# The second MLP's u turned by transposing DMAs, as two planes of 16-bit halves, in a two-layer decoder trunk on one Trainium2 core

## The chip, the core and the metric

The kernel runs on one core of one Trainium2 chip. The core has five engines that work at the same time, each through its own list of instructions in order: TensorE (PE, matrix products; its weight loads are listed apart as PEld), VectorE (DVE), ScalarE (ACT), GpSimd (POOL) and SyncE (SP), which here issues the DMAs. An instruction that needs another engine's result waits for a semaphore, and everything behind it on its engine waits too. Data lies in SBUF (128 partitions); TensorE writes its sums to PSUM, which ScalarE and VectorE can read and a DMA cannot.

The metric is the time of one execution on the device in microseconds (us); lower is better. A profiled execution is one execution with its trace: when each instruction ran, and what it waited for.

## The reference

Two layers work on x (256 tokens x 2048 features, float32). Layer 0 mixes tokens with a convolution module, layer 1 with differential attention; each is followed by the same kind of MLP with hidden width 8192. The change touches the MLP of layer 1 alone:

```python
def squared_relu_mlp(h, w1, b1, w2, b2):
    u = jnp.square(jax.nn.relu(h @ w1 + b1))
    return u @ w2 + b2
...
    for i in range(DEPTH):
        ...
        x = layer_norm(DEEPNORM_ALPHA * x + g_m * y, ln_mix_g[i], ln_mix_b[i])
        h = x * (1.0 + sc_f) + sh_f
        y = squared_relu_mlp(h, mlp_w1[i], mlp_b1[i], mlp_w2[i], mlp_b2[i])
        x = layer_norm(DEEPNORM_ALPHA * x + g_f * y, ln_ffn_g[i], ln_ffn_b[i])
```

The scales, shifts and gates (sc, sh, g) come from an adaptive layer norm: products of a condition vector with the rows of a large matrix (`ada_w`), which the kernel computes in between, on VectorE.

## The kernel before

**Products.** Each large product is made of three: both factors are split into a high part that TensorE multiplies at full speed (type fp32r) and a low part, the rest. high x high, high x low and low x high are summed in PSUM (lines 700, 702 and 703). The weights come from HBM in tiles of 1 MB (2048 numbers on each of the 128 partitions, line 636). A tile is worked on in two halves of 1024: ScalarE casts a half to its high part `wh` (line 655), VectorE subtracts to get the low part `wl` (line 657), and TensorE does 12 matmuls with it (2 blocks of 128 rows, 2 blocks of 128 tokens, 3 products). There are four buffers for raw tiles (`N_RAW`), shared with the rows of the adaLN matrix, and four pairs of buffers for split halves (`N_SP`).

**The MLP** (`mlp`, called with i = 1 for the second). The hidden width is worked on in four quarters q. A quarter has four groups g of w1 (512 hidden columns each, 4 tiles, 8 halves), which fill u for this quarter, and then four groups n of w2, each over the quarter's 2048 rows (again 4 tiles, 8 halves). A group's sum lies in two PSUM banks, one for each block of 128 tokens, t = 0 and 1.

**Turning u.** A w1 group leaves u with tokens on the partitions; w2 needs it with hidden features there. When a bank of a w1 group is done, `on_t1` runs: ScalarE copies it to SBUF (`us`, line 1452), and `rest` is put off by `U_WAIT` = 2 ticks. Then TensorE makes four 128x128 transposes into a PSUM bank (`ut`, line 1458). In the second MLP VectorE adds the bias b1 (line 1471) and makes the square of the positive part (line 1474), both to `r`; ScalarE casts `r` to u's high part (`u_hi`, line 513) and VectorE subtracts for the low part (`u_lo`, line 516), in `put_split`. Both u buffers hold a whole quarter.

**What sets the order.** `run_jobs` writes the program half by half. Before the matmuls of a half it fetches the half four further on (`AHEAD`): its cast and its subtraction. After each half comes a `tick`; what `defer(n, f)` put off runs when its tick is reached. From this a scheduler makes each engine's final order by its own estimate of times; the order of instructions on an engine is fixed from then on. Weight loads, loads of adaLN rows and all else that SP issues stand in one list.

In q = 0 of the second MLP, row blocks of the adaLN matrix are loaded and multiplied beside the weights (lines 419 and 228).

Of the kernel before, what the change touches and what calls it, by code (L numbers as in the profile page):

```python
# [11 lines left out]
F32 = mybir.dt.float32  # L12
F32R = mybir.dt.float32r
I32 = mybir.dt.int32
AF = mybir.ActivationFunctionType
ALU = mybir.AluOpType
AX = mybir.AxisListType
# [2 lines left out]
P = 128  # L20
# [5 lines left out]
NG = 512  # L26
# [21 lines left out]
AHEAD = 4  # L48
POOL_LO = ()
U_WAIT = 2  # L50
POOL_LEAD = ()
POOL_TAIL = ()
GF_LOAD = 16
# [27 lines left out]
def group_order(s):  # L81

    return list(range(NGRP))[::1 if (len(SLICES) - s) % 2 else -1]
# [72 lines left out]
def trunk(  # L156
# [8 lines left out]
    nc = tc.nc  # L165
# [5 lines left out]
    work = ctx.enter_context(tc.tile_pool(name="work", bufs=2))  # L171
# [10 lines left out]
    def tp_tile(name):  # L182
        return ps_tp[0].tile([P, 512], F32, tag="tp", name=name)
# [20 lines left out]
    cond = const.tile([P, KC], F32, name="cond")  # L204
    nc.scalar.activation(cond, cT, AF.Sigmoid)
    nc.vector.tensor_tensor(cond, cond, cT, op=ALU.mult)
# [34 lines left out]
    def defer(n, fn):  # L241
        put_off.append((ticks[0] + n, fn))
# [265 lines left out]
    def put_split(pair, c0, n, s0, ns, src, eng=None, trail=False):  # L508

        hi, lo = pair  # L510
        h = hi[:, c0:c0 + n, s0:s0 + ns]
        l = lo[:, c0:c0 + n, s0:s0 + ns]
        nc.scalar.copy(h, src)  # L513

        def low():
            (eng or nc.vector).tensor_tensor(l, src, h.bitcast(F32), op=ALU.subtract)  # L516
        if trail:
            trailing.append(low)
        else:
            low()  # L520

    def chunk_h(mul, add, c0, n, between=None):

        h32 = [work.tile([P, 1, S], F32, tag="B", name=f"h0_h{c0 + j}") for j in range(n)]
        for j in range(n):
# [4 lines left out]
            else:  # L530
                nc.scalar.activation(h32[j][:, 0, :], xT[:, cc, :], AF.Identity,
                                     scale=mul[:, cc:cc + 1], bias=add[:, cc:cc + 1])
# [6 lines left out]
    def feat_t(src, pair, mul, add, t, name):  # L539

        def block(b):
# [6 lines left out]
            for j in range(4):  # L548
                cc = 4 * b + j
                if b in ACT_B:  # L550
                    nc.scalar.activation(h32[:, j, :], pt[:, j * P:(j + 1) * P], AF.Identity,
                                         scale=mul[:, cc:cc + 1], bias=add[:, cc:cc + 1])
# [54 lines left out]
    def add_group(key, pair, srcs, lead=False, tail=False, pump=None, start=None, pre_t=None, on_t=None,  # L607
# [7 lines left out]
        for blk in blocks:  # L615
# [6 lines left out]
            for i in blk:  # L622
                for q in range(2):
                    pool = ((lead and 2 * i + q in POOL_LEAD) or (tail and 2 * (i - len(srcs)) + q in POOL_TAIL)
                            or 2 * i + q in on_pool)
# [173 lines left out]
    def normalise(src, t, mv, rs, nb, js=range(4), on_act=False):  # L799
        for j in js:  # L800
            sl = slice(j * NG, (j + 1) * NG)
            if on_act:
                nc.scalar.activation(src[:, t, sl], src[:, t, sl], AF.Identity, scale=rs, bias=nb)
            else:
# [133 lines left out]
    def conv_out(j, n):  # L938
        cs[j]["v", n] = work.tile([P, S], F32, tag="S", name=f"vpe_{j}_{n}", bufs=3)
        nc.scalar.activation(cs[j]["v", n], cs[j]["ps", n][:, :S], AF.Identity,  # L940
                             bias=cv["dwb"][:, 2 * j + n:2 * j + n + 1])
# [14 lines left out]
    def glu(j):  # L956
# [12 lines left out]
        for cc in range(2):  # L969
            ch = 2 * j + cc  # L970
            sg = work.tile([P, S], F32, tag="S", name=f"sg_{j}_{cc}", bufs=3)
            nc.scalar.activation(sg, pg[:, cc * S:(cc + 1) * S], AF.Sigmoid,
                                 bias=cv["pw1b"][:, KC + ch:KC + ch + 1], scale=1.0)
# [11 lines left out]
    for g in range(NGRP):  # L985
# [3 lines left out]
    cv = {}  # L989

    cv.update(pw1b=vec1[:, 96:128], dwb=vec1[:, 128:144], clng=vec1[:, 144:160], clnb=vec1[:, 160:176],
              b1c=vec1[:, 176:304], lnc=vec1[:, 304:432], subg=vec1[:, 432:434])
# [137 lines left out]
    rest = [cond_quarter(q, tp_tile(f"cond_p{q}")) for q in (2, 3)]  # L1130
# [129 lines left out]
    for s, (f0, nf) in enumerate(SLICES):  # L1260
# [6 lines left out]
        for pos, k in units:  # L1267
            g = group_order(s)[pos]
# [3 lines left out]
            if (s, h) in X_AT:  # L1272
                a, b = X_AT[s, h]
# [8 lines left out]
            if nf > 1 or pos % 2 == 0:  # L1282
                parts = w_parts.pop(0)
# [14 lines left out]
            if not last and h >= END_AT[s]:  # L1298
                n = h - END_AT[s] - 1 + (s + 1 < BOTH_PE)
# [105 lines left out]
    for q in range(4):  # L1405
        defer(4 + q, lambda q=q: alpha_x(q))

    def mlp(i, ln_g, ln_b, gcol, bcol, pump, at_end, start=None, mid=None, last=None):
        gate, sc, cur = {}, {}, {}
        st = stats_tile(f"mlp{i}")  # L1410

        def begin():
            if start is not None:
                start()
            cur["hT"] = hT_pair("hT", f"hm{i}")
            base_x(ln_g, None, f"basem{i}", 18, 4)

        def prep():
            need((i, SC_F), (i, SH_F))
            sc["mul"], sc["add"] = h_scalars(gcol, bcol, mods[(i, SC_F)], mods[(i, SH_F)], ALPHA, f"hm{i}")  # L1420

        def pre_t(t):
            return feat_t(z, cur["hT"], sc["mul"], sc["add"], t, f"hm{i}")

        def start_gate():
            need((i, G_F))
            gate["gb"] = gate_bcast(mods[(i, G_F)], f"gbm{i}")
            defer(1, start_base)

        def start_base():  # L1430
            base_bias(mods[(i, G_F)], cv["lnc"][:, 96 + KC * i:96 + KC * (i + 1)], bcol, f"basem{i}", 4)

        def begin_q(q):
            if q == 0:
                begin()
            if q == 2 and mid is not None:
                mid()
            cur["uT"] = hT_pair("uT", f"u{i}_{q}")

        def begin_w2(q):  # L1440
            if q == 0:
                defer(5, start_gate)
            if q == 3 and last is not None:
                last["begin"]()

        for q in range(4):
            for g in range(4):
                n0 = q * D + g * NG

                def on_t1(t, ps, q=q, g=g, n0=n0):  # L1450
                    us = work.tile([P, NG], F32, tag="A", name=f"us_{i}_{q}_{g}_{t}")
                    nc.scalar.copy(us, ps)
                    uT = cur["uT"]

                    def rest():
                        pt = tp_tile(f"ut_{i}_{q}_{g}_{t}")
                        for j in range(4):
                            nc.tensor.transpose(out=pt[:, j * P:(j + 1) * P], in_=us[:, j * P:(j + 1) * P],  # L1458
                                                identity=ident)
                        r = work.tile([P, 4, P], F32, tag="B", name=f"r_{i}_{q}_{g}_{t}")  # L1460
                        f0 = i * 64 + n0 // P
                        if i == 0:
                            for j in range(4):
                                nc.scalar.activation(r[:, j, :], pt[:, j * P:(j + 1) * P], AF.Relu,
                                                     bias=cv["b1c"][:, f0 + j:f0 + j + 1])
                            if q == 0:
                                nc.scalar.activation(r, r, AF.Square)
                            else:
                                nc.vector.tensor_tensor(r, r, r, op=ALU.mult)
                        else:  # L1470
                            nc.vector.tensor_tensor(r, pt.rearrange("p (a n) -> p a n", a=4),
                                                    cv["b1c"][:, f0:f0 + 4].unsqueeze(2).broadcast_to([P, 4, P]),
                                                    op=ALU.add)
                            nc.vector.scalar_tensor_tensor(r, r, 0.0, r, ALU.max, ALU.mult)
                        put_split(uT, g * 4, 4, t * P, P, r, trail=True)
                    defer(U_WAIT, rest)
                first = q == 0 and g == 0
                add_group(f"w1_{i}_{q}_{g}", lambda: cur["hT"], wtiles(mlp_w1[i], 0, KC, n0), pump=pump, lead=(i + 1) * first,
                          start=(lambda q=q: begin_q(q)) if g == 0 else None,
                          pre_t=pre_t if first else None, on_t=on_t1, prep=(i == 1, prep) if first else None,  # L1480
                          between=ada_between if first and i == 0 else None)
            for n in range(4):
                def on_t2(t, ps, q=q, n=n):
                    add_gated(ps, gate["gb"], t, n, f"w2g_{i}_{q}_{n}_{t}")
                    if q == 3:
                        nc.vector.bn_stats(st[t][:, n, :], z[:, t, n * NG:(n + 1) * NG])
                        if n == 3:
                            return at_end(st, t)
                        if last is not None and t == 1 and n in (1, 2):
                            last["product"](t, n)  # L1490
                add_group(f"w2_{i}_{q}_{n}", lambda: cur["uT"], wtiles(mlp_w2[i], q * KC, KC, n * NG), pump=pump,
                          start=(lambda q=q: begin_w2(q)) if n == 0 else None,
                          tail=(q == 3 and n == 3) * (2 if last is None else 3), on_t=on_t2)
# [35 lines left out]
    def attn_tables():  # L1529
        posi = small.tile([P, NT], I32, tag="posi", name="posi", bufs=1)  # L1530
        with tc.issue_after(raws["dma"].ins):
# [347 lines left out]
```

## Time and profile before

| | |
|---|---|
| median of 3 runs | 2283.74 us (2283.18 to 2287.07) |
| the profiled execution | 2285.3 us, of which the span of its trace is 2282.2 |
| granted TensorE clock | 0.996 |
| VectorE, ScalarE busy | 1718.6 us (75%), 1080.6 us (47%) |
| moved by DMA | 608.57 MB, mean 267 GB/s |
| second MLP | its first w1 group ends on TensorE at about 1582 us of the span |

How to read the rows: a group of instructions is written as line, engine, operation, out<-in by the program's names without buffer numbers, shapes, how many, then busy time in us and mean ns of one, then the time the engine stood idle just before them and what ended it. In a timeline a row begins with the start in us from the span's start and the duration; xN says that N neighbours are merged, and the bracket gives the idle time before and its releaser. A row of DMA issues ends with the KB of one and the median us from issue to landing. `w_ps` is a PSUM bank of a weight product, `hm` is the MLP's input and `u` its hidden layer, each with `hi` and `lo`.

The change moves no load of weights and no matmul of a product; it takes one kind of instruction off TensorE and puts others on ScalarE and on SP's list.

### The profile page before, as it was taken

What the parts mean: (1) busy time and instruction counts of PE and PEld (TensorE: products, weight loads), DVE (VectorE), ACT (ScalarE), POOL (GpSimd) and SP (SyncE); (2) the same over time, 40 slices, a digit from 0 to 9 for tenths busy, and PEclk for the clock granted to TensorE, in tenths of its full rate; (3) what the DMA queues carried; (4) which work ended last, traced back from release to release, by engine and by line L of the source; (5) the groups of instructions that cost most, each with busy time, mean ns of one, the idle gap of its engine ahead of it and who ended that gap; (6) DMA issues with size and microseconds to landing.
All of it is one profiled execution on the core that took longest, in us unless ns stands there. A gap on an engine that the chain in (4) does not pass through costs nothing.

```text
span 2282.2 us, 28177 instructions
## 1 busy us (share of the span) xinstructions
PE 2242.6 (98%) x11060; PEld 1796.5 (79%) x11060; DVE 1718.6 (75%) x2120; ACT 1080.6 (47%) x1487; POOL 52.1 (2%) x58
## 2 busy tenths in 40 slices
PE   8999999999999999999999999999999999999999
PEld 5677657688888888888878888877888888888887
DVE  7687989778978888777878877887866555655666
ACT  4336863564355355355454445535434444443442
POOL 0000001000000000000000010100000000000000
PEclk9999999999999999999999999999999999999999
DMA  9996789699988988988757766774966556556563
GB/s 395 420 392 257 312 328 370 217 340 337 345 304 306 316 291 307 324 292 309 280 176 248 240 221 211 272 273 162 336 228 196 184 189 199 182 187 199 188 222 111
DMA packets 217473, 608.57 MB, mean 267 GB/s; under 512 B 10382, under 2 KB 10610, under 8 KB 187770
## 3 DMA queue, kind: packets, MB, share of 16 engines
q1 hardware_dynamic: 217340, 606.78, 74.8%
q8 instruction: 86, 1.41, 0.3%
q14 instruction: 47, 0.39, 0.0%
HBM read 604.59 MB, written 2.15 MB: 266 GB/s over the span
## 4 chain that ended last, share of the span: by engine, by line
PE 85%; DVE 6%; issue 3%; DMA 2%; ACT 2%; POOL 0%; SPq 0%; ACTq 0%; DVEq 0%; POOLq 0%
PE w_ps L703 20%; PE w_ps L700 20%; PE w_ps L702 20%; PE pw_ps L598 2%; PE pw_ps L599 2%; PE pw_ps L600 2%; PE qkv_q_ps L703 1%; PE qkv_q_ps L700 1%; PE ut L1458 1%; PE qkv_k_ps L703 1%; PE qkv_k_ps L700 1%; PE qkv_q_ps L702 1%; PE qkv_v_ps L703 1%; PE qkv_v_ps L700 1%; PE qkv_k_ps L702 1%
## 5 line engine op out<-in xcount | busy, mean ns | idle before, releaser
L657 DVE TENSOR_TENSOR wl_w<-w_w,wh_w 128x1024 fp32r<-128x1024 f32 x510 | 614.7, 1222 | 330.1 <-ACT wh_w L655 329.7
L655 ACT CAST wh_w<-w_w 128x1024 fp32r<-128x1024 f32 x512 | 535.3, 1054 | 691.2 <-PE w_ps L703 520.3
L700 PE MATMUL w_ps<-wh_w,hm_hi 128*128 128x512 f32 x1024 | 402.5, 393 | 1.9 <-ACT hm_hi L513 1.9
L703 PE MATMUL w_ps<-wh_w,hm_lo 128*128 128x512 f32 x1024 | 400.2, 391 | 1.6 <-DVE hm_lo L516 1.6
L702 PE MATMUL w_ps<-wl_w,u_hi 128*128 128x512 f32 x1024 | 399.0, 390 | 1.3 <-DVE wl_w L657 1.3
L702 PE MATMUL w_ps<-wl_w,hm_hi 128*128 128x512 f32 x1024 | 399.6, 390 | 0.0
L700 PE MATMUL w_ps<-wh_w,u_hi 128*128 128x512 f32 x1024 | 399.5, 390 | 0.0
L703 PE MATMUL w_ps<-wh_w,u_lo 128*128 128x512 f32 x1024 | 398.5, 389 | 0.0
L228 DVE SCALAR_TENSOR_TENSOR adaw<-adaw,cond_rows 128x2048 f32<-128x2048 f32 x108 | 246.7, 2284 | 1.0 <-DMA adaw<-in_ada_rows_dram 1.0
L700 PEld LDWEIGHTS w_ps<-wh_w,hm_hi 128*128 128x128 f32 x1024 | 193.0, 188 | 43.6 <-ACT hm_hi L513 3.5
L703 PEld LDWEIGHTS w_ps<-wh_w,hm_lo 128*128 128x128 f32 x1024 | 192.9, 188 | 43.1 <-DVE hm_lo L516 2.9
L702 PEld LDWEIGHTS w_ps<-wl_w,u_hi 128*128 128x128 f32 x1024 | 192.2, 188 | 42.5 <-DVE wl_w L657 2.9
L702 PEld LDWEIGHTS w_ps<-wl_w,hm_hi 128*128 128x128 f32 x1024 | 193.0, 188 | 39.2
L700 PEld LDWEIGHTS w_ps<-wh_w,u_hi 128*128 128x128 f32 x1024 | 192.2, 188 | 40.0
L703 PEld LDWEIGHTS w_ps<-wh_w,u_lo 128*128 128x128 f32 x1024 | 192.2, 188 | 39.9
L598 PE MATMUL pw_ps<-wh_pw,h_hi 128*128 128x512 f32 x256 | 103.2, 403 | 3.5 <-DVE vtok L1113 1.7
L599 PE MATMUL pw_ps<-wl_pw,h_hi 128*128 128x512 f32 x256 | 100.2, 391 | 0.9 <-DVE wl_pw L583 0.8
L600 PE MATMUL pw_ps<-wh_pw,h_lo 128*128 128x512 f32 x256 | 100.0, 390 | 0.0
L583 DVE TENSOR_TENSOR wl_pw<-w_pw,wh_pw 128x1024 fp32r<-128x1024 f32 x64 | 77.2, 1220 | 28.4 <-ACT wh_pw L580 28.2
L580 ACT CAST wh_pw<-w_pw 128x1024 fp32r<-128x1024 f32 x64 | 65.8, 1050 | 46.4 <-PE pw_ps L600 27.2
L598 PEld LDWEIGHTS pw_ps<-wh_pw,h_hi 128*128 128x128 f32 x256 | 48.0, 188 | 30.8 <-issue 13.8
L516 DVE TENSOR_TENSOR u_lo<-r,u_hi 128x512 fp32r<-128x512 f32 x64 | 43.6, 688 | 18.2 <-ACT u_hi L513 16.9
(351 smaller groups left out, 3007.0 us busy)
## 6 DMA issues: line engine op xcount, KB each, us to landing
w_w<-in_mlp_w_dram SPq DMA_DIRECT2D x256, 1024.0 KB, 5.6
adaw<-in_ada_rows_dram SPq DMA_DIRECT2D x108, 1024.0 KB, 6.7
w_pw<-in_pw_tiles_dram SPq DMA_DIRECT2D x32, 1024.0 KB, 11.6
ad<-in_ada_rows_dram SPq DMA_DIRECT2D x25, 1024.0 KB, 8.3
w_pw<-in_conv_pw_w_dram SPq DMA_DIRECT2D x16, 1024.0 KB, 7.4
w_qkv_q<-in_attn_qkv_w_dram SPq DMA_DIRECT2D x16, 1024.0 KB, 5.1
w_qkv_k<-in_attn_qkv_w_dram SPq DMA_DIRECT2D x16, 1024.0 KB, 5.1
w_qkv_v<-in_attn_qkv_w_dram SPq DMA_DIRECT2D x16, 1024.0 KB, 6.5
```

Source lines behind the costliest of these rows:

```text
L228: nc.vector.scalar_tensor_tensor(w, w, 1.0, cond_rows, ALU.mult, ALU.mult, accum_out=m[:, ch:ch + 1])
L516: (eng or nc.vector).tensor_tensor(l, src, h.bitcast(F32), op=ALU.subtract)
L580: nc.scalar.copy(hq, rq)
L583: nc.vector.tensor_tensor(lq, rq, hq.bitcast(F32), op=ALU.subtract)
L598: nc.tensor.matmul(pss[t], lhsT=xh, rhs=wh, start=(kc == first), stop=False)
L599: nc.tensor.matmul(pss[t], lhsT=xh, rhs=wl, start=False, stop=False)
L600: nc.tensor.matmul(pss[t], lhsT=xl, rhs=wh, start=False, stop=(kc == last))
L655: nc.scalar.copy(hi, rq)
L657: eng.tensor_tensor(lo, rq, hi.bitcast(F32), op=ALU.subtract)
L700: nc.tensor.matmul(pss[tt], lhsT=xh, rhs=wh, start=(kc == 0 and job["bias"] is None), stop=False)
L702: nc.tensor.matmul(pss[tt], lhsT=xh, rhs=wl, start=False, stop=False)
L703: nc.tensor.matmul(pss[tt], lhsT=xl, rhs=wh, start=False, stop=(kc == nk - 1))
```

## The change

In the MLP of layer 1 all 32 blocks of u (16 groups, 2 blocks of tokens) are turned without TensorE. A transposing DMA moves elements of 16 bits, so `halves_t` takes a float32 number as two:

- ScalarE copies the PSUM bank as 16-bit numbers into two planes, `uh` (all halves b = 0, then all halves b = 1; 1024 elements on each partition). It takes the place of the copy `us`.
- SP issues one DMA for each block that transposes the eight 128x128 squares of `uh` into `ux`. It waits for the copy.
- `rest` is put off by `T_WAIT` = 4 ticks instead of 2. ScalarE copies `ux` with the planes interleaved again into `r`, which is float32 once more.
- VectorE adds the bias in place and makes the square as before; the cast and the subtraction to u's high and low part are the old ones.

The 128 transposes on TensorE and their PSUM banks are gone there. All buffers come from pools that exist already (tags A, C and B).

```diff
+T_WAIT = 4
...
+    def by_dma(i, q, g):
+        return i == 1
+
+    def halves_t(t, ps, uT, i, q, g, n0):
+
+        name = f"{i}_{q}_{g}_{t}"
+        parts = work.tile([P, 2, NG], U16, tag="A", name=f"uh_{name}")
+        nc.scalar.copy(parts.rearrange("p b n -> p n b"), ps.bitcast(U16).rearrange("p (n b) -> p n b", b=2))
+        turned = work.tile([P, 2, 4, P], U16, tag="C", name=f"ux_{name}")
+        nc.sync.dma_start_transpose(turned.rearrange("p b a n -> p (b a) n"), parts.rearrange("p b n -> p (b n)"))
+
+        def rest():
+            r = work.tile([P, 4, P], F32, tag="B", name=f"r_{name}")
+            nc.scalar.copy(r.rearrange("p a n -> p (a n)").bitcast(U16).rearrange("p (a n b) -> p a n b", a=4, b=2),
+                           turned.rearrange("p b a n -> p a n b"))
+            f0 = i * 64 + n0 // P
+            nc.vector.tensor_tensor(r, r, cv["b1c"][:, f0:f0 + 4].unsqueeze(2).broadcast_to([P, 4, P]), op=ALU.add)
+            nc.vector.scalar_tensor_tensor(r, r, 0.0, r, ALU.max, ALU.mult)
+            put_split(uT, g * 4, 4, t * P, P, r, trail=True)
+        defer(T_WAIT, rest)
...
                 def on_t1(t, ps, q=q, g=g, n0=n0):
+                    uT = cur["uT"]
+                    if by_dma(i, q, g):
+                        return halves_t(t, ps, uT, i, q, g, n0)
                     us = work.tile([P, NG], F32, tag="A", name=f"us_{i}_{q}_{g}_{t}")
                     nc.scalar.copy(us, ps)
-                    uT = cur["uT"]
```

On TensorE the pairs of `ut` rows of the second MLP are left out and nothing else moves. On ScalarE and VectorE the u work stands later. Here is ScalarE's order before, from the end of the first w1 group of quarter 1. The digits of `wh_w_1_1_1_2_0` are: w1, layer 1, quarter 1, group 1, tile 2, half 0; so tile and half 1_1 are half 3 of the next group, 2_0 half 4, and so on.

```order
L1452 COPY us_1_0_0_14087<-w_1_1_0_ps_13949 128x512
L1452 COPY us_1_0_1_14089<-w_1_1_0_ps_13950 128x512
L655 CAST wh_w_1_1_1_1_1_14093<-w_w_1_1_1_1_14069 128x1024
L655 CAST wh_w_1_1_1_2_0_14131<-w_w_1_1_1_2_14129 128x1024
L513 CAST u_1_hi<-r_1_0_0_14114 128x4x128
L513 CAST u_1_hi<-r_1_0_1_14123 128x4x128
L655 CAST wh_w_1_1_1_2_1_14147<-w_w_1_1_1_2_14129 128x1024
```

The same place with the change (its own line numbers: 657 is the cast, 515 the high part):

```order
L1417 COPY uh_1_0_0_14071<-w_1_1_0_ps_13933 128x512x2
L1417 COPY uh_1_0_1_14075<-w_1_1_0_ps_13934 128x512x2
L657 CAST wh_w_1_1_1_1_1_14081<-w_w_1_1_1_1_14053 128x1024
L657 CAST wh_w_1_1_1_2_0_14099<-w_w_1_1_1_2_14097 128x1024
L1423 COPY r_1_0_0_14131<-ux_1_0_0_14073 128x1024
L1423 COPY r_1_0_1_14136<-ux_1_0_1_14077 128x1024
L657 CAST wh_w_1_1_1_2_1_14115<-w_w_1_1_1_2_14097 128x1024
L657 CAST wh_w_1_1_1_3_0_14145<-w_w_1_1_1_3_14143 128x1024
L515 CAST u_1_hi<-r_1_0_0_14131 128x4x128
L657 CAST wh_w_1_1_1_3_1_14161<-w_w_1_1_1_3_14143 128x1024
L515 CAST u_1_hi<-r_1_0_1_14136 128x4x128
```

The r copies, which wait for the DMAs, now stand where the high parts stood, ahead of the cast of half 5, and the high parts moved behind the casts of halves 6 and 7. VectorE at the same place, before:

```order
L657 TENSOR_TENSOR wl_w_1_1_1_1_1_14094<-w_w_1_1_1_1_14069,wh_w_1_1_1_1_1_14093 128x1024
L1471 TENSOR_TENSOR r_1_0_0_14114<-ut_1_0_0_14109,vec_101 128x512
L1474 SCALAR_TENSOR_TENSOR r_1_0_0_14114<-r_1_0_0_14114 128x512
L1471 TENSOR_TENSOR r_1_0_1_14123<-ut_1_0_1_14118,vec_101 128x512
L1474 SCALAR_TENSOR_TENSOR r_1_0_1_14123<-r_1_0_1_14123 128x512
L516 TENSOR_TENSOR u_1_lo<-r_1_0_0_14114,u_1_hi 128x4x128
L516 TENSOR_TENSOR u_1_lo<-r_1_0_1_14123,u_1_hi 128x4x128
L657 TENSOR_TENSOR wl_w_1_1_1_2_0_14132<-w_w_1_1_1_2_14129,wh_w_1_1_1_2_0_14131 128x1024
```

VectorE with the change (659 is the subtraction, 518 the low part):

```order
L659 TENSOR_TENSOR wl_w_1_1_1_2_1_14116<-w_w_1_1_1_2_14097,wh_w_1_1_1_2_1_14115 128x1024
L1426 TENSOR_TENSOR r_1_0_0_14131<-r_1_0_0_14131,vec_101 128x512
L1427 SCALAR_TENSOR_TENSOR r_1_0_0_14131<-r_1_0_0_14131 128x512
L1426 TENSOR_TENSOR r_1_0_1_14136<-r_1_0_1_14136,vec_101 128x512
L1427 SCALAR_TENSOR_TENSOR r_1_0_1_14136<-r_1_0_1_14136 128x512
L518 TENSOR_TENSOR u_1_lo<-r_1_0_0_14131,u_1_hi 128x4x128
L518 TENSOR_TENSOR u_1_lo<-r_1_0_1_14136,u_1_hi 128x4x128
L659 TENSOR_TENSOR wl_w_1_1_1_3_0_14146<-w_w_1_1_1_3_14143,wh_w_1_1_1_3_0_14145 128x1024
```

The six u operations moved from between halves 3 and 4 to between halves 5 and 6. In quarter 0 the order differs a little from group to group; this is ScalarE after the first w1 group with the change:

```order
L1423 COPY r_0_0_0_12853<-ux_0_0_0_12789 128x1024
L1423 COPY r_0_0_1_12858<-ux_0_0_1_12793 128x1024
L657 CAST wh_w_1_0_1_2_1_12834<-w_w_1_0_1_2_12816 128x1024
L657 CAST wh_w_1_0_1_3_0_12867<-w_w_1_0_1_3_12865 128x1024
L657 CAST wh_w_1_0_1_3_1_12883<-w_w_1_0_1_3_12865 128x1024
L515 CAST u_0_hi<-r_0_0_0_12853 128x4x128
L657 CAST wh_w_1_0_2_0_0_12901<-w_w_1_0_2_0_12899 128x1024
L515 CAST u_0_hi<-r_0_0_1_12858 128x4x128
```

Here the second high part stands behind the cast of the first half of the group after (half 8, counted on), while VectorE again has both low parts between the subtractions of halves 5 and 6. On SP the two transposing DMAs of a group stand between two weight loads, those of tiles 0 and 1 of the group after the next.

More of the change, by code (lines that the diff above doesn't have):

```diff
@@ L14 @@
 I32 = mybir.dt.int32
+U16 = mybir.dt.uint16
 AF = mybir.ActivationFunctionType
```

## The prediction

> **What bounds the kernel now.** I first read the page's busy line, then a table of stretches over the second MLP, where the change lies. The first two stretches of the table are its first quarter (q = 0: four w1 groups, then four w2 groups); the others lie in q = 1 to 3.
>
> ```profile
> PE 2242.6 (98%) x11060; PEld 1796.5 (79%) x11060; DVE 1718.6 (75%) x2120; ACT 1080.6 (47%) x1487; POOL 52.1 (2%) x58
> ```
> ```profile
> 1581.70:1671.50 89.80, 89.80 (x415) 74.61 (x414) 74.97 (x83) 42.07 (x49) 0.00 (x0) 1.00 0.83 292
> 1671.50:1760.00 88.50, 88.50 (x393) 73.18 (x392) 54.95 (x57) 34.26 (x34) 0.00 (x0) 1.00 0.65 217
> 1760.00:1850.00 90.00, 90.00 (x415) 74.85 (x414) 53.80 (x56) 42.17 (x48) 0.00 (x0) 1.00 0.58 184
> 1850.00:2025.00 175.00, 175.00 (x790) 145.27 (x789) 102.39 (x104) 75.22 (x79) 0.00 (x0) 1.00 0.59 192
> ```
>
> The columns are length, then busy time of PE, PEld, DVE, ACT and POOL, the granted clock, the DMA share and GB/s. TensorE is busy in every microsecond and the clock is 1.00: an instruction taken off TensorE shortens the span, as long as nothing else becomes late. VectorE has 14.8 us free of 89.8 in the w1 part of q = 0, and 36 of 90 later. So the questions are how much TensorE time goes, and whether the new way of u, through ScalarE, a DMA, ScalarE and VectorE, holds up a weight that TensorE needs.
>
> **What is removed.** The next rows are the timeline around one pair of transposes, and the starts of u's copies by ScalarE, one pair for each w1 group.
>
> ```profile
> 1985.62 0.39 PE L703 MATMUL w_ps<-wh_w,hm_lo 128*128 128x512 f32 x1
> ...
> 1985.86 1.03 PE L1458 MATMUL ut<-ident,us 128*128 128x128 f32 x8
> ...
> 1986.64 0.48 PE L700 MATMUL w_ps<-wh_w,hm_hi 128*128 128x512 f32 x1
> ```
> ```profile
> 1805.00 1.27 ACT L1452 COPY us<-w_ps 128x512 f32<-128x512 f32 x2 [0.98 <-PE w_ps L703]
> ...
> 1827.65 1.27 ACT L1452 COPY us<-w_ps 128x512 f32<-128x512 f32 x2 [0.98 <-PE w_ps L703]
> ...
> 1937.34 1.27 ACT L1452 COPY us<-w_ps 128x512 f32<-128x512 f32 x2 [0.98 <-PE w_ps L703]
> ```
> ```profile
> 1859.14 1.05 ACT L655 CAST wh_w<-w_w 128x1024 fp32r<-128x1024 f32 x1 [1.67 <-PE w_ps L703]
> 1861.86 1.05 ACT L655 CAST wh_w<-w_w 128x1024 fp32r<-128x1024 f32 x1 [1.67 <-PE w_ps L703]
> ```
> ```profile
> 1860.23 1.22 DVE L657 TENSOR_TENSOR wl_w<-w_w,wh_w 128x1024 fp32r<-128x1024 f32 x1 [1.50 <-ACT wh_w L655]
> ```
>
> A half of a weight tile is 12 matmuls; ScalarE's cast of the half four further on waits for the buffer that this frees, so the casts' distance is the half's time: 2.72 us, 0.227 for each matmul, and 21.76 for a group of eight halves without transposes. A w1 group with one pair of transposes takes 1827.65 - 1805.00 = 22.65. The difference is 0.89. The second way gives the same: 1827.65 to 1937.34 is five groups of which one holds a pair, 109.69 - 5 x 21.76 = 0.89. Sixteen groups give **16 x 0.89 = 14.2 us**, which is all that the change can bring.
>
> **What is added**, with the duration of the nearest row; all are of the second MLP (the window also holds the tail of attention).
>
> ```profile
> L657 DVE TENSOR_TENSOR wl_w<-w_w,wh_w 128x1024 fp32r<-128x1024 f32 x255 | 308.9, 1223 | 238.2 <-ACT wh_w L655 238.1
> L655 ACT CAST wh_w<-w_w 128x1024 fp32r<-128x1024 f32 x256 | 268.6, 1053 | 350.6 <-PE w_ps L703 309.5 <-issue 20.6 <-DMA w_w<-in_mlp_w_dram 13.1
> ...
> L1474 DVE SCALAR_TENSOR_TENSOR r<-r 128x512 f32<-128x512 f32 x32 | 22.2, 692 | 1.1
> ...
> L1471 DVE TENSOR_TENSOR r<-ut,vec 128x512 f32<-128x512 f32 x32 | 22.0, 687 | 4.7 <-PE ut L1458 4.7
> ...
> L516 DVE TENSOR_TENSOR u_lo<-r,u_hi 128x512 fp32r<-128x512 f32 x32 | 21.9, 688 | 1.8 <-ACT u_hi L513 0.6
> L513 ACT CAST u_hi<-r 128x512 fp32r<-128x512 f32 x32 | 19.7, 621 | 20.8 <-DVE r L1474 20.8
> L1452 ACT COPY us<-w_ps 128x512 f32<-128x512 f32 x32 | 18.7, 588 | 16.1 <-PE w_ps L703 14.8
> ```
>
> ScalarE: the copy out of PSUM now moves 1024 halves instead of 512 words; the row with 1024 elements is the weight cast, 1.05 us, so 0.46 more than 0.588. The new copy that puts r together is 1024 elements too, 1.05. No row has 16-bit elements: by element count 1.05, from below 0.59 (if a pair went as one word), from above 2.1 (if each 2-byte write cost two); I take 1.05, since both copies have the cast's count. Together 2 x (0.46 + 1.05) = 3.0 us a group, where ScalarE works 42 of 90 us: hidden as work, not necessarily as a wait. VectorE: the bias addition reads SBUF instead of PSUM, 0.688 in u_lo's row against 0.687; nothing.
>
> The 32 transposing DMAs are new, 256 KB each, and no row shows one. Neighbours in size and place:
>
> ```profile
> w_w<-in_mlp_w_dram SPq DMA_DIRECT2D x122, 1024.0 KB, 5.2
> ...
> out_dram<-z SPq DMA_DIRECT2D x8, 256.0 KB, 2.0
> basem_gb<-in_ln_mix_g_dram SPq DMA_DIRECT2D x4, 256.0 KB, 5.9
> ...
> basem_b<-basem_d SPq DMA_DIRECT2D x4, 256.0 KB, 4.2
> ```
>
> From issue to landing a 256 KB DMA takes 2.0 us on a quiet queue (out_dram, also out of SBUF), 4.2 beside weight loads, 5.9 in the crowded q = 0. I take 4 (nearest to basem_b), with 2.0 and 5.9 as ends; if the two of a group ran strictly one after the other at 5.9, they would end 11.8 after the first issue. A sentence of the Trainium skill stands beside this: "Advanced Engine Details and Errata", section X-Bar Transpose (TRN2), calls transposing DMAs as fast as regular ones, 350 to 400 GB/s; by that the two would move 256 KB each in 0.7 us (an estimate), and land like out_dram. No run here shows it yet.
>
> **When must they land?** Call E the moment when TensorE ends a w1 group, and number the halves of the next group from 0 (the next group of the last is the first of w2). The cast of half k is free when half k - 4 is done, at E + 2.72 (k - 3). The order of the change's instructions, shown above, decides: VectorE does wl of half 5, then all six u operations, then half 6; ScalarE does half 4, the two r copies, then half 5. Back from TensorE: half 6 starts at E + 6 x 2.72 = 16.3. Ahead of it, one after another: second r copy 1.05, cast of half 5 1.05, its wl 1.22, four VectorE operations 2.76, two lo parts 1.38, wl of half 6 1.22: 8.7, and some 0.3 for six handoffs (the cast quoted above ends at 1859.14 + 1.05 = 1860.19 and its wl starts at 1860.23; I use 0.05 each). **The second transposing DMA must land by E + 7.3.** The copies out of PSUM start 0.5 before E (us starts at 1982.65; half 0's twelfth matmul, the first row above, at 1985.62, so its first at 1983.13):
>
> ```profile
> 1982.65 1.27 ACT L1452 COPY us<-w_ps 128x512 f32<-128x512 f32 x2 [0.98 <-PE w_ps L703]
> ```
>
> They end at E + 0.6 and E + 1.7; landing at 4 us gives E + 5.7, 1.6 us to spare; at 5.9 it is 0.3 late. The other wait of this order, lo's second part on hi's, which stands behind the cast of half 7 (free at E + 10.9), ends with wl of half 6 at 10.9 + 1.05 + 0.62 + 0.69 + 1.22 = 14.5: in time. Of a weight load that happens to be in the queue ahead, the spare swallows most; I charge 2 us for all twelve groups of q = 1 to 3. For the last group of a quarter, u's last chunk is also read by half 6 of w2, at the same E + 16.3, and its lo is ready ahead of wl 6.
>
> On SP the two DMAs wait for ScalarE, and the next weight load behind them waits too. SP waits anyway:
>
> ```profile
> SPq L636 <- DVE wl_w L657: 551.1, 115, 8.1
> ```
>
> A load's buffer comes free about when VectorE has done half 3 of the next group, E + 4; four buffers of two halves mean that its first cast comes at E + 19; 5.2 us of flight leave 9.8. Nothing, unless the two hold SP for 10 us.
>
> **q = 0 is worse.** There ScalarE's order puts the second hi of the first group behind the cast of half 8, which is free at E + 5 x 2.72 = 13.6: 13.6 + 1.05 + 0.62 + 0.69 + 1.22 and four handoffs is 17.4, about 0.9 after half 6's second matmul (16.55) wants wl. In the other three groups VectorE also has adaLN products between, with only 14.8 us free in 89.8, and the DMA share is 0.83:
>
> ```profile
> L228 DVE SCALAR_TENSOR_TENSOR adaw<-adaw,cond_rows 128x2048 f32<-128x2048 f32 x15 | 34.3, 2285 | 0.0
> ```
>
> One such product is 2.3 us; I charge somewhat over half of one, 1.4, to each of the three: 0.9 + 4.2 = 5.1 us, between 0.9 (the first group alone) and 15 (landings by 5.9 after one another).
>
> **The sum**: 14.2 - 5.1 - 2 = 7.1 us less. The profiled execution took 2285.3 us (span 2282.2 and 3.1 around it): 2278.2. The median shown, 2283.74, is 1.6 lower, so I forecast **2277** (2283.74 - 7.1 = 2276.6).
>
> **Rivals.**
> - *Even*: the stalls eat the gain. With the landing 0.3 late in q = 1 to 3 (5.9 us) the twelve groups lose 3.6 instead of 2, and q = 0 loses 8 to 10 instead of 5: 2281 to 2283. For it: the only rows of 256 KB beside other traffic are 4.2 and 5.9. Against: 5.9 comes from the stretch with share 0.83, and the others have 0.58 to 0.65.
> - *Late landing, slower*: ScalarE stands at its r copy, behind it the cast of half 5, and each microsecond after E + 7.3 stops TensorE once a group: 16 us per microsecond. It decides from 0.45 us late (7.1 / 16). Two microseconds late give 2277 + 32 = 2309; both DMAs in turn at 5.9 (E + 12.4, 5.1 late) give 2277 + 82 = 2359. For it: nothing in the trace tells how fast a transposing DMA is, and two stand in a row. Against: 1 MB lands in 5.2.
> - *Slow 16-bit copies, slower*: at 2.1 us each the copies end at E + 3.8 instead of 1.7 and r's costs 1.05 more, so E + 7.8 stands against a due time of 6.2: 1.6 late, 2277 + 26 = 2303. Against: 1024 elements, as in the cast.
> - *Block by block, slower*: if a DMA's eight blocks of 128 columns went one after another at no less than a quarter of the 2.0 row each, a DMA would take 4 us and the pair E + 8.6, 1.3 late, 2298; at the full 2.0 each the pair lands at E + 32.6, longer than a group, and sixteen times the 25 us excess is 2677. The Trainium skill speaks for this: "VectorE: DVE Perf Modes", section The three transpose paths, gives 390 ns for a 128x128 16-bit transpose on TensorE and 1309 on the DMA path, and keeps TensorE wherever PSUM will do; by its figure, blocks in turn, a DMA would take 10.5 us (an estimate). TensorE's eight here took 0.89 together by the rows above, far below 390 each.
>
> **Chances.** Forecast (faster, its own range 2270 to 2279) 0.50; even 0.20; late landing 0.20; slow copies 0.05; block by block 0.05. Changes under about 0.2% (4.6 us) can't be told from none here. Faster 0.50, the same 0.20, slower 0.30. The range runs from 2270 (all 14.2 us) to 2308 (landing two microseconds late); about 0.12 lies above, 0.03 below.
>
> **What would show it.** Right: no L1458 row in the second MLP; w1 groups of q = 1 to 3 at 21.8 us; VectorE's r L1426 waiting for ScalarE without TensorE waiting; transposing DMAs landing 3 to 5 us after issue. Wrong: TensorE waiting for wl_w of half 6 once in each group (late landing), ScalarE's r L1423 waiting for ux over 2 us, L1417 or L1423 above 1.3 us, or SP's loads late.

## The result and the profile after

| | before | after |
|---|---|---|
| median | 2285.4 us (2283.18 to 2287.68, 4 runs) | 2360.58 us (2359.44 to 2362.78, 4 runs) |
| ratio | | 1.0329, 95% interval 1.0316 to 1.0342 |
| profiled execution, its span | 2285.3, 2282.2 us | 2361.1, 2359.0 us |
| granted TensorE clock | 0.996 | 0.986 |

The kernel became 75 us slower, where 2277 was forecast. The page's busy line after:

```profile
PE 2263.5 (96%) x10932; PEld 1795.9 (76%) x10932; DVE 1713.6 (73%) x2120; ACT 1240.3 (53%) x1519; POOL 52.3 (2%) x58
```

128 transposes are gone (11060 - 10932), and TensorE is nevertheless busy 21 us longer. ScalarE is busy 160 us longer; the forecast's 3.0 us a group, sixteen times, would be 48. Which of its instructions it is, the groups by line over the second MLP (and the tail of attention) show, in the columns of before:

```profile
L659 DVE TENSOR_TENSOR wl_w<-w_w,wh_w 128x1024 fp32r<-128x1024 f32 x252 | 301.6, 1221 | 315.0 <-ACT wh_w L657 315.0
L657 ACT CAST wh_w<-w_w 128x1024 fp32r<-128x1024 f32 x252 | 264.7, 1069 | 260.3 <-PE w_ps L705 241.8 <-DMA w_w<-in_mlp_w_dram 16.8 <-DVE wl_w L659 1.7
...
L1417 ACT COPY uh<-w_ps 128x1024 uint16<-128x1024 uint16 x32 | 151.8, 5002 | 15.2 <-PE w_ps L705 15.2
...
L1423 ACT COPY r<-ux 128x1024 uint16<-128x1024 uint16 x32 | 36.9, 1167 | 4.4 <-DMA ux<-uh 4.4
```

The copy `uh` takes **5.0 us**, nearly five times the 1.05 of a cast with as many elements. It is about the same for all 32, which the tile's own view says (shortest, median, longest in ns), with the transposing DMAs' hold on SP and their way from issue to landing:

```profile
L1417 ACT COPY uh<-w_ps x32: 4830/5024/5179, 1584.5 to 2260.5; 128x1024 uint16<-128x1024 uint16 x32
L1419 SPq DMA_TRANSPOSE ux<-uh x32: 1232/1235/2353, 1589.3 to 2265.7; - x32
...
DMA to landing us min/median/max: 3.0/3.0/3.2
```

TensorE's waits from 1560 us to the end (total, how often, longest; before, the wait for `wl` was 1.3 us in all):

```profile
PE w_ps L704 <- DVE wl_w L659: 30.0, 27, 4.5
PE w_ps L702 <- ACT wh_w L657: 27.9, 17, 2.6
```

How the copy becomes these waits is seen in one group of q = 2: ScalarE's timeline, then the TensorE rows that begin with a wait.

```profile
1985.13 9.48 ACT L1417 COPY uh<-w_ps 128x1024 uint16<-128x1024 uint16 x2 [0.98 <-PE w_ps L705]
1994.12 2.29 ACT L657 CAST wh_w<-w_w 128x1024 fp32r<-128x1024 f32 x2
1996.31 1.17 ACT L1423 COPY r<-ux 128x1024 uint16<-128x1024 uint16 x1
1997.71 1.17 ACT L1423 COPY r<-ux 128x1024 uint16<-128x1024 uint16 x1 [0.23 <-DMA ux<-uh]
...
2011.42 4.83 ACT L1417 COPY uh<-w_ps 128x1024 uint16<-128x1024 uint16 x1 [0.94 <-PE w_ps L705]
```
```profile
1995.52 0.50 PE L702 MATMUL w_ps<-wh_w,hm_hi 128*128 128x512 f32 x1 [1.58 <-ACT wh_w L657]
1996.78 0.50 PE L704 MATMUL w_ps<-wl_w,hm_hi 128*128 128x512 f32 x1 [0.76 <-DVE wl_w L659]
...
2006.51 0.50 PE L704 MATMUL w_ps<-wl_w,hm_hi 128*128 128x512 f32 x1 [1.28 <-DVE wl_w L659]
```

The group before ends at E = 1985.6. The two copies hold ScalarE until 1994.6, E + 9.0. The cast of half 3 stands behind them; TensorE wants it at E + 3 x 2.72 = 1993.8, gets it late and waits 1.58, then 0.76 for the `wl` made from it. The second DMA goes out at 1994.6 and lands 3.0 later, the r copies follow, and `wl` of half 6 is late by 1.28. The group takes 2011.42 - 1985.13 = 26.29 us, against 21.76 for its matmuls alone and 22.65 before. The last wait decides: TensorE gets the `wl` of half 6 at 2006.5, E + 20.9, and would want it at E + 16.55 (half 6's second matmul), which is 4.4 of the 4.53 us that the group is longer than its matmuls. The two earlier waits fall within this delay and add nothing to it.

The starts of `uh`, and of `us` before, divide the whole loss. First after, then before (the rows of q = 1 stand in the prediction):

```profile
1584.46 9.48 ACT L1417 COPY uh<-w_ps 128x1024 uint16<-128x1024 uint16 x2 [0.98 <-PE w_ps L705]
...
1680.01 9.48 ACT L1417 COPY uh<-w_ps 128x1024 uint16<-128x1024 uint16 x2 [0.97 <-PE w_ps L705]
1792.95 9.48 ACT L1417 COPY uh<-w_ps 128x1024 uint16<-128x1024 uint16 x2 [0.98 <-PE w_ps L705]
```
```profile
1581.74 1.27 ACT L1452 COPY us<-w_ps 128x512 f32<-128x512 f32 x2 [0.98 <-PE w_ps L703]
...
1649.70 1.27 ACT L1452 COPY us<-w_ps 128x512 f32<-128x512 f32 x2 [0.98 <-PE w_ps L703]
1759.65 1.27 ACT L1452 COPY us<-w_ps 128x512 f32<-128x512 f32 x2 [0.98 <-PE w_ps L703]
```

Three group distances of q = 0 take 95.55 us instead of 67.96 (27.6 more). Then come thirteen passes, the four quarters' last groups and the nine w1 groups of q = 1 to 3, each 3.0 to 3.7 longer (112.94 instead of 109.95 after q = 0; 26.29 instead of 22.65): 46.5 in all. The first group ended 2.7 later, ahead of the change's first instruction. Together 76.8, the difference of the spans.

The table of stretches, its first and third row as shown of before, where both had 1.00 as the clock and full TensorE time:

```profile
1581.70:1671.50 89.80, 71.16 (x281) 54.90 (x279) 55.48 (x61) 59.81 (x41) 0.00 (x0) 0.94 0.73 237
...
1760.00:1850.00 90.00, 84.01 (x359) 67.97 (x358) 44.23 (x45) 58.11 (x42) 0.00 (x0) 0.98 0.59 185
```

The granted clock is now below 1.00 as well. The theory after this view, **copy**: `uh` alone makes the loss, and the rest of the change is as cheap as forecast. Its rivals: the transposing DMAs or the later order of u's operations make it as well; and, on why the copy is slow, reading PSUM as 16 bits (R), writing half words (P), or the way the writes jump (J, later D and L).

### The profile page after: what moved, and what is told of

The parts are those of the page before. It is cut to its first block, busy times and chain, and to the rows that moved or that the text cites. A ratio compares the mean times of both kernels' runs of the same rounds, so it can differ in the third digit from the quotient of the medians.

```text
span 2359.0 us, 28059 instructions
## 1 busy us (share of the span) xinstructions
PE 2263.5 (96%) x10932; PEld 1795.9 (76%) x10932; DVE 1713.6 (73%) x2120; ACT 1240.3 (53%) x1519; POOL 52.3 (2%) x58
## 4 chain that ended last, share of the span: by engine, by line
PE 69%; DVE 10%; ACT 9%; DMA 6%; issue 5%; POOL 0%; SPq 0%; ACTq 0%; DVEq 0%; POOLq 0%
PE w_ps L704 16%; PE w_ps L705 15%; PE w_ps L702 15%; ACT uh L1417 4%; DVE wl_w L659 2%; DMA w_w<-in_mlp_w_dram 2%; PE cv L936 2%; ACT wh_w L657 2%; PE pw_ps L600 2%; PE pw_ps L601 1%; PE pw_ps L602 1%; DMA conv_ux<-in_ada_tiles_dram 1%; PE qkv_v_ps L705 1%; PE qkv_v_ps L702 1%; PE qkv_v_ps L704 1%
## 5 line engine op out<-in xcount | busy, mean ns | idle before, releaser
L704 PE MATMUL w_ps<-wl_w,hm_hi 128*128 128x512 f32 x1024 | 407.9, 398 | 25.4 <-DVE wl_w L659 25.4
L702 PE MATMUL w_ps<-wh_w,hm_hi 128*128 128x512 f32 x1024 | 408.0, 398 | 24.1 <-ACT wh_w L657 21.6
L705 PE MATMUL w_ps<-wh_w,hm_lo 128*128 128x512 f32 x1024 | 405.6, 396 | 1.6 <-DVE hm_lo L518 1.6
L1417 ACT COPY uh<-w_ps 128x1024 uint16<-128x1024 uint16 x32 | 151.8, 5002 | 15.2 <-PE w_ps L705 15.2
```

Of the source, the lines that this page charges most:

```text
L702: nc.tensor.matmul(pss[tt], lhsT=xh, rhs=wh, start=(kc == 0 and job["bias"] is None), stop=False)
L704: nc.tensor.matmul(pss[tt], lhsT=xh, rhs=wl, start=False, stop=False)
L705: nc.tensor.matmul(pss[tt], lhsT=xl, rhs=wh, start=False, stop=(kc == nk - 1))
L1417: nc.scalar.copy(parts.rearrange("p b n -> p n b"), ps.bitcast(U16).rearrange("p (n b) -> p n b", b=2))
```

## The experiments

**1. The same copy with the planes written densely.** The elements are the same; the walk goes along a plane instead of across the two, so that the jumps are on the reading side.

```diff
-nc.scalar.copy(parts.rearrange("p b n -> p n b"), ps.bitcast(U16).rearrange("p (n b) -> p n b", b=2))
+nc.scalar.copy(parts, ps.bitcast(U16).rearrange("p (n b) -> p b n", b=2))
```

> Same numbers and places, but ScalarE walks one plane after the other: it reads every second 16-bit element of the PSUM bank and writes 1024 elements densely. Theory W (the write pattern costs: each 16-bit element written lies 1 KB from the one before, about 4.9 ns for each): uh falls from 5.0 us to about 1.1, the stalls of TensorE go, and the kernel takes what was forecast for the change, 2270 to 2280 us. Theory R (16-bit reads out of PSUM cost): uh stays near 5 us and the kernel near 2360 us.

Measured 2282.86 us against 2286.46, ratio 0.9985 (0.9976 to 0.9994). Its tile view, and ScalarE's timeline at two groups of q = 1:

```profile
L1417 ACT COPY uh<-w_ps x32: 1012/1014/1017, 1579.8 to 2179.1; 128x1024 uint16<-128x1024 uint16 x32
L1419 SPq DMA_TRANSPOSE ux<-uh x32: 1243/1278/5728, 1580.8 to 2181.7; - x32
...
DMA to landing us min/median/max: 3.1/3.2/5.1
```
```profile
1764.80 1.93 ACT L1417 COPY uh<-w_ps 128x1024 uint16<-128x1024 uint16 x2 [0.98 <-PE w_ps L705]
1786.56 1.93 ACT L1417 COPY uh<-w_ps 128x1024 uint16<-128x1024 uint16 x2 [0.94 <-PE w_ps L705]
```

The copy falls from 5.0 to 1.01 us, and 75 us of loss turn into a gain of 3.6: it was the copy. A group of q = 1 now takes 21.76, the matmuls' time to the hundredth, so the whole 0.89 is gained there. Yet the total gains 3.6 us and not 14. The missing part is in q = 0, in the same timeline and SP's:

```profile
1579.77 1.93 ACT L1417 COPY uh<-w_ps 128x1024 uint16<-128x1024 uint16 x2 [0.98 <-PE w_ps L705]
...
1643.94 2.00 ACT L657 CAST wh_w<-w_w 128x1024 fp32r<-128x1024 f32 x2 [5.72 <-DMA w_w<-in_mlp_w_dram]
...
1655.47 1.93 ACT L1417 COPY uh<-w_ps 128x1024 uint16<-128x1024 uint16 x2 [0.99 <-PE w_ps L705]
```
```profile
1604.19 6.82 SPq L1419 DMA_TRANSPOSE ux<-uh  x2
```

Three group distances take 75.7 instead of 3 x 21.76 = 65.3: 10.4 us lost, with casts waiting up to 5.72 for weight loads.

**2. Is it the read from PSUM?** The bank is copied whole to SBUF first, and split from there with jumping writes as in the change.

```diff
+us = work.tile([P, NG], F32, tag="X", name=f"us_{name}", bufs=3)
+nc.scalar.copy(us, ps)
-nc.scalar.copy(parts.rearrange("p b n -> p n b"), ps.bitcast(U16).rearrange("p (n b) -> p n b", b=2))
+nc.scalar.copy(parts.rearrange("p b n -> p n b"), us.bitcast(U16).rearrange("p (n b) -> p n b", b=2))
```

> ScalarE first copies the bank to SBUF as 512 words (0.59 us, as before the change) and then splits it into planes from there, with the same jumping writes as the change. Theory W: the split stays at about 5 us and the kernel is at 2360 us or above. Theory R: the split takes about 1.2 us like the copy that puts r together, and the kernel takes 2275 to 2295 us.

```profile
L1419 ACT COPY uh<-us x32: 4867/4871/4925, 1592.1 to 2265.2; 128x1024 uint16<-128x1024 uint16 x32
```

2362.75 us in one run; the split takes 4.87 us from SBUF too. The side that is read, PSUM or not, is not the cause.

**3. Words in, dense half words out.** Both planes receive the bank rounded to bfloat16; the copy reads 32-bit words and has no jump on either side.

```diff
-nc.scalar.copy(parts.rearrange("p b n -> p n b"), ps.bitcast(U16).rearrange("p (n b) -> p n b", b=2))
+nc.scalar.copy(parts.bitcast(mybir.dt.bfloat16), ps.unsqueeze(1).broadcast_to([P, 2, NG]))
```

> Leaves out the split into halves: both planes get the bank rounded to 16-bit floats, by 32-bit reads out of PSUM and dense 16-bit writes of 1024 elements; all that follows is as in the change. Both theories W and R: about 1.05 us for the copy and 2270 to 2280 us. If 16-bit writes as such were slow, the copy would stay near 5 us and the kernel near 2360 us.

2284.99 us, ratio 0.9995 (0.9986 to 1.0005), the copy 1.015 us (1.012 to 1.018). So in 1 the jumping reads cost nothing measurable. The expected 2270 to 2280 was missed, for q = 0 stalls here as in 1: its three group distances take 74.3, 9.0 us lost.

**4. The dense copy, and the new way only in q = 1 to 3.** q = 0 keeps TensorE's transposes.

```diff
-        return i == 1
+        return i == 1 and q > 0
...
+nc.scalar.copy(parts, ps.bitcast(U16).rearrange("p (n b) -> p b n", b=2))
```

> Dense planes as in e1, and the first quarter keeps TensorE's transposes. If e1's w1 groups of q = 1 to 3 run at 21.8 us because nothing waits there, and its 7.7 us of loss are all in q = 0 (weight loads that land late behind the transposing DMAs, and u's operations in front of wl), then 12 x 0.89 = 10.7 us are left: 0.9953 of before, some 2275 us. If the gain of q = 1 to 3 were given back elsewhere, the ratio would be that of e1, 0.9985.

**2274.54 us** (2271.47 to 2277.26, 5 runs) against 2285.9, ratio 0.9956 (0.9943 to 0.9970): 0.44% faster than the kernel before. The table of stretches, q = 0's w1 groups and a part of q = 1, TensorE without a gap in either:

```profile
1581.70:1671.50 89.80, 89.80 (x415) 74.55 (x414) 75.91 (x83) 40.91 (x48) 0.00 (x0) 1.00 0.84 291
1760.00:1850.00 90.00, 90.00 (x399) 74.53 (x398) 57.94 (x62) 54.19 (x56) 0.00 (x0) 1.00 0.70 211
```

Twelve groups at 0.89 are 10.7 us; measured 11.4.

**5. Do jumping 32-bit writes cost the same?** In the kernel before, `us` is written alternately to two halves of its buffer, 1 KB apart; the bank is read in the same jumping order.

```diff
+nc.scalar.copy(us.rearrange("p (b n) -> p n b", b=2), ps.rearrange("p (b n) -> p n b", b=2))
```

> The kernel before with one thing changed: the copy us of the second MLP walks the two halves of the 512 words alternately, on both sides (each word written lies 1 KB from the one before; the result is the same). Theory J (the jump costs whatever the width): 512 x 4.9 ns = 2.5 us for the copy instead of 0.59. Theory P (only writes of part of a 32-bit word cost): 0.6 us, and the kernel's time is that of before.

```profile
L1455 ACT COPY us<-w_ps x32: 560/589/591, 457.0 to 1062.4; 128x512 f32<-128x512 f32 x32
L1453 ACT COPY us<-w_ps x32: 1092/1132/1205, 1583.1 to 2185.2; 128x512 f32<-128x512 f32 x32
```

1.13 us instead of 0.59 (first MLP, unchanged): neither the 2.5 of theory J nor the 0.6 of P. The kernel takes 2286.47 us in one run, as before the edit. A jump costs a word 1.06 ns more (0.543 us by 512), a half word in `uh` about 3.9 (5.00 - 1.01 us by 1024).

**6. Half words written 4 bytes apart.** As 4, but the copy to `r` reads the planes densely and writes every second half word of `r`, then the others.

```diff
-nc.scalar.copy(r.rearrange("p a n -> p (a n)").bitcast(U16).rearrange("p (a n b) -> p a n b", a=4, b=2),
-               turned.rearrange("p b a n -> p a n b"))
+nc.scalar.copy(r.rearrange("p a n -> p (a n)").bitcast(U16).rearrange("p (a n b) -> p b a n", a=4, b=2),
+               turned)
```

> e4 with the copy that puts r together walked the other way round: it reads each plane densely and writes every second 16-bit element of r (4 bytes apart). Theory J: no jump to another region, so about 1.2 us as now (1.17). Theory P: each write is half a word whose other half does not follow at once, so about 5 us, and the kernel slower than e4 by some 40 to 60 us.

```profile
L1423 ACT COPY r<-ux x24: 1335/1356/1366, 1772.7 to 2192.7; 128x1024 uint16<-128x1024 uint16 x24
```

1.36 us instead of 1.17. Half words written by themselves, each word touched twice, are thus not slow as such: P falls. (One run of 2281.87; from the first transposing DMA to the end the two traces take the same, 510.8 and in experiment 4 510.7, so what differs lies ahead of the edit.)

**7. The slow copy alone.** The kernel before with TensorE's transposes, and after each `us` a jumping split of it that nobody reads.

```diff
+parts = work.tile([P, 2, NG], U16, tag="C", name=f"uh_{i}_{q}_{g}_{t}")
+nc.scalar.copy(parts.rearrange("p b n -> p n b"),
+               us.bitcast(U16).rearrange("p (n b) -> p n b", b=2))
```

> The kernel before, with TensorE's transposes and all, plus one more copy of us into two planes in the jumping order, whose result nothing reads. Theory W (the slow copy by itself made the loss): 4.9 us for each copy, w1 groups at about 26 to 27 us instead of 22.7, 2350 to 2380 us. If the loss needed the DMAs or the later order, it stays within 10 us of before.

Its waits of TensorE, same window as above:

```profile
PE ut L1463 <- ACT us L1453: 35.0, 16, 3.3
PE w_ps L703 <- DVE wl_w L658: 10.5, 8, 1.4
```

2350.45 us in one run, 64.5 more than before, without any transposing DMA and with the old order of u's operations. Its w1 groups of q = 1 to 3 take 26.6 to 26.7 us. Two such copies a group are enough to stop TensorE, though here on another path: first at its transposes, whose `us` for the second block stands behind the first split.

**8. Which jumps are slow?** Eight patterns of that unread split, one for each quarter and block of tokens. `blocks(m)` writes single half words alternately to two places 2m bytes apart, `runs(m)` runs of m half words alternately to two places 1 KB apart; the last pattern is the change's.

```diff
+def blocks(m):
+    return (parts.rearrange("p (c b m) -> p c m b", b=2, m=m), half.rearrange("p (c m b) -> p c m b", b=2, m=m))
+def runs(m):
+    return (parts.rearrange("p (b c m) -> p c b m", b=2, m=m), half.rearrange("p (c m b) -> p c b m", b=2, m=m))
```

> The kernel before plus one extra copy of us for each block, whose result nothing reads, in eight walking orders (16-bit, 1024 elements each): alternating between two places 32, 64, 128, 256 or 1024 bytes apart (control), and 1024 bytes apart with runs of 2, 4 or 16 elements. Theory D (distance: 16-bit writes near each other are gathered before they reach SBUF, those that jump are not, and a lone half word then costs a read and a write): about 1.2 us at the short distances, 4.9 at 1024 bytes, with the step at some distance between; runs of 2 (whole words) give 2.2 us, as e5's words do (1.13 for 512), runs of 16 about 1.2. Theory L (the length of the inner run, 2 elements, costs by itself): 4.9 us at every distance, and runs of 2 the same.

The groups by line; in this order 64 bytes apart, 1 KB (the change's), 32 bytes, 256 bytes, then runs of 2 and of 4:

```profile
L1468 ACT COPY uh<-us 128x1024 uint16<-128x1024 uint16 x4 | 20.0, 4997 | 0.0
L1480 ACT COPY uh<-us 128x1024 uint16<-128x1024 uint16 x4 | 19.6, 4902 | 0.0
L1466 ACT COPY uh<-us 128x1024 uint16<-128x1024 uint16 x4 | 19.6, 4902 | 0.1
...
L1472 ACT COPY uh<-us 128x1024 uint16<-128x1024 uint16 x4 | 19.6, 4897 | 0.0
...
L1474 ACT COPY uh<-us 128x1024 uint16<-128x1024 uint16 x4 | 4.5, 1131 | 0.1
...
L1476 ACT COPY uh<-us 128x1024 uint16<-128x1024 uint16 x4 | 4.2, 1042 | 0.0
```

All single writes are slow, 4.85 to 5.0 us, from 32 bytes on (the kernel took 2326.53 us in one run): the step that theory D looked for is not in this range. Runs of two already cost 1.13, so L, which had them as slow as single ones, falls too. What the runs leave standing is a bare rule: a half word whose neighbour in its word is not written next, with the next write 32 bytes or more away, costs ScalarE 4.7 to 4.9 ns instead of about 1. Where between 4 and 32 bytes this begins, and what does it, is open.

**9. What stalls q = 0?** Experiment 4, and in q = 0 dense splits and transposing DMAs that nobody reads; TensorE's transposes and the old order stay.

```diff
+if i == 1:
+    parts = work.tile([P, 2, NG], U16, tag="C", name=f"uh_{i}_{q}_{g}_{t}")
+    nc.scalar.copy(parts, us.bitcast(U16).rearrange("p (n b) -> p b n", b=2))
+    turned = work.tile([P, 2, 4, P], U16, tag="X", name=f"ux_{i}_{q}_{g}_{t}", bufs=3)
+    nc.sync.dma_start_transpose(turned.rearrange("p b a n -> p (b a) n"), parts.rearrange("p b n -> p (b n)"))
```

> e4 (q = 1 to 3 by DMA, q = 0 by TensorE), and in q = 0 also the dense copy to planes and the transposing DMAs, whose result nothing reads: the load on ScalarE, SP and the DMA queue without the later order of u's operations. Theory Q (the DMA queue and SP behind the transposing DMAs make weights late): q = 0's four group ends lie at least 4 us further apart than e4's 67.96 us, as e1's do (75.7). Theory O (it is the order, u's operations in front of wl): 67.96 us within 1.5.

The table of stretches, SP's timeline, and ScalarE's:

```profile
1581.70:1671.50 89.80, 84.10 (x382) 68.35 (x381) 70.83 (x78) 45.70 (x53) 0.00 (x0) 1.00 0.95 291
```
```profile
1612.83 6.11 SPq L1483 DMA_TRANSPOSE ux<-uh  x2
```
```profile
1636.91 1.04 ACT L657 CAST wh_w<-w_w 128x1024 fp32r<-128x1024 f32 x1 [6.95 <-DMA w_w<-in_mlp_w_dram]
```

2283.26 us in one run. Three group distances of q = 0 (the first `us` starts at 1584.58, the last at 1659.76) take 75.2 instead of 67.96: 7.2 us lost with u's old order, by casts that wait for weight loads. The DMA share is 0.95 where 4 has 0.84. So transposing DMAs between the loads, with the splits that feed them, are enough for 7.2 us, where 1 lost 10.4. Whether it is SP, held up to 6 us by a pair with the loads behind it, or the DMA engines' time, these runs don't separate.

## Why the prediction was wrong

- **The step that failed** is the price of the `uh` copy: "by element count 1.05, from below 0.59 (if a pair went as one word), from above 2.1 (if each 2-byte write cost two); I take 1.05, since both copies have the cast's count". It measured 5.0, more than twice the upper bound. The element count was carried from a dense row to a copy that writes single half words to two places in turn. The copy to `r`, for which the same value was taken, jumps only in its reads and measured 1.17. A sentence of the Trainium skill has the same gap: "ScalarE: Activation LUTs", section What ACT_TABLE_LOAD costs, gives an activation instruction a fixed part of 186 ns and then one element a cycle, 0.833 ns for each, fp32 and bf16 alike; for 1024 elements that is 1.04 us (an estimate). The dense copy agrees (1.01 us); 5.0 us does not.
- *Slow 16-bit copies* was the right rival with the wrong size and 0.05 as its chance. At 2.1 it gave 2303; the measured durations by the same steps give: copies end at E + 9.0, landing at E + 9.0 + 3.0 = 12.0, due at 7.3 less 0.1 for the longer r copy. That is 4.8 late, and sixteen times this less 14.2 is 63. The trace shows 4.53 lost in each group of q = 1 to 3, and 46.5 us in the thirteen passes after q = 0's groups, for which these steps give 51. The three distances of q = 0 lost 27.6 where the steps give 12; there the casts also wait for weight loads. Another 2.7 lies ahead of the change.
- **The due time**, E + 7.3 and from there each microsecond once a group, held, and so did the place, `wl` of half 6: 4.4 us late by the trace, 4.8 by these steps. It was not the first place. The casts of half 3 and 4 stand behind the copies too, and that of half 3 was late first (E + 8.5 against a need before E + 8.16). The prediction asked only what waits for the DMA, not what waits behind the copy itself. Here that added nothing, but experiment 7 shows that the copy can stop TensorE without any landing.
- **What is removed**, 0.89 a group, was right: 21.76 in experiments 1 and 4, and 11.4 us for twelve groups.
- **The landing** at 4 us was on the safe side (3.0 to 3.2 in the change, 5.1 at most in experiment 1). *Block by block* falls: eight blocks land in 3.0 us together. By the 1309 ns a block of "VectorE: DVE Perf Modes", section The three transpose paths, in the Trainium skill it would have been 10.5 (an estimate); the trace shows less than a third. *Late landing* came true as an event, but because the copy ended late, not because the DMA was slow. Its 2359 lies beside the measured 2360.58 by chance: it stands for two DMAs of 5.9 in turn, 5.1 late, where two copies of 5.0 made the landing 4.8 late.
- **q = 1 to 3**, charged 2 us: nothing, once the copy is dense.
- **q = 0**, charged 5.1 with bounds of 0.9 and 15: 10.4 in experiment 1. The causes named were the order of u's operations and VectorE's adaLN products. What the runs show is chiefly another one, which the prediction had set aside ("Nothing, unless the two hold SP for 10 us"): a pair held SP for up to 6.8 us while each load was short of time already. In the stretch of 9 the clock was 1.00 and in 1 it was 0.96; 0.04 of 89.8 us is 3.6, about what separates 10.4 from 7.2. Experiment 3, with the order of 1, lost 9.0 at a clock of 0.98 (0.02 of 74.3 is 1.5, which leaves 7.5). This fits the clock better than the order of u's operations, but neither was tried by itself.
- Without the copy's price the forecast would have been off by 6 us: 2283 in experiment 1, and *even* as the outcome.

## What to carry to other kernels

Price a copy by the pattern that it writes, not by its element count: put the jumps on the reading side, and where a split needs 16-bit pieces, write each plane densely. Ask of a longer instruction what stands behind it on its own engine, as well as who waits for its result. A DMA added to the list that issues the weights was free here where loads had slack (q = 1 to 3) and cost 7.2 us where they had little (q = 0), so such a change is worth trying stage by stage.

## What the hardware showed

- ScalarE, 1024 half words on each of 128 partitions: dense 1.01 us; jumping reads from SBUF 1.17; writes 4 bytes apart 1.36; runs of two, 1 KB apart, 1.13; single writes 32 bytes to 1 KB apart 4.85 to 5.0.
- A transposing DMA of 256 KB holds SP for 1.24 us in the median, and 5.7 at most in experiment 1; it lands 3.0 to 3.2 after issue. In the stretch from 1760 us experiment 4 has a DMA share of 0.70 where before has 0.58: 0.12 x 90 us for eight of them (four groups), 1.35 us of all 16 engines each. That is an upper bound, for the stretch moves 2.4 MB more, of which the eight are 2.1; without the loads' part about 1.2 is left. A weight load of 1 MB, by share and bytes of before (0.58 for 184 GB/s), is 3.3, or 0.8 for 256 KB. "Advanced Engine Details and Errata", section X-Bar Transpose (TRN2), in the Trainium skill has the two equally fast; here they differ by a factor of about 1.5.
- After a wait TensorE can also run slower. In q = 0 of the change, after a wait of 3.43 us, the rows show the matmuls 0.43 us apart instead of 0.23, eight times in turn, and a granted clock of 0.56 in these 6 us (the columns are those of the table of stretches):

```profile
1672.00:1678.00 6.00, 4.73 (x13) 3.74 (x14) 5.83 (x7) 1.19 (x3) 0.00 (x0) 0.56 0.86 290
```
```profile
1673.27 0.80 PE L704 MATMUL w_ps<-wl_w,hm_hi 128*128 128x512 f32 x1 [3.43 <-DVE wl_w L659]
1673.87 0.63 PE L705 MATMUL w_ps<-wh_w,hm_lo 128*128 128x512 f32 x1
1674.30 0.63 PE L702 MATMUL w_ps<-wh_w,hm_hi 128*128 128x512 f32 x1
```

Shorter waits can be enough. In the change's q = 1, in the group that begins at 1819 us, waits of 1.58 and 0.76 us are followed by the same spacing and a clock of 0.74. Around the same two waits in the group of q = 2 shown above, the clock stayed at 1.00:

```profile
1828.00:1834.00 6.00, 3.66 (x9) 2.69 (x9) 2.41 (x3) 5.78 (x7) 0.00 (x0) 0.74 0.55 139
...
1995.00:2001.00 6.00, 4.72 (x20) 3.68 (x21) 3.49 (x3) 5.55 (x6) 0.00 (x0) 1.00 0.74 207
```
```profile
1829.63 0.50 PE L702 MATMUL w_ps<-wh_w,hm_hi 128*128 128x512 f32 x1 [1.58 <-ACT wh_w L657]
1830.89 0.80 PE L704 MATMUL w_ps<-wl_w,hm_hi 128*128 128x512 f32 x1 [0.76 <-DVE wl_w L659]
```

What decides between the two is not shown. In these groups the slower matmuls cost nothing of their own: the one of q = 1 takes 26.32 us against 26.29, and the third wait, for the `wl` of half 6, is missing in it.
